# Sums of weights by adding transfers in three units of an output projection

## The chip, the cores and the metric

The kernel runs on one core of a Trainium2 chip. The metric is the device time of one execution in microseconds (us), as the median of a few runs. Beside it stands one execution that was recorded instruction by instruction; every duration below comes from that record. Engines are named as the profile names them: PE multiplies matrices (PEld loads its weights), DVE is the vector engine, ACT the scalar engine, POOL the GpSimd engine, SP the engine that does nothing here but issue transfers. Transfers from SP stand in queue q1, those from POOL in queue q0, and both are carried out by the same 16 DMA engines. A transfer issued from POOL can add to what lies in its destination instead of overwriting it; here it is called an adding transfer.

## The reference, cut to what matters

Two layers on a sequence of 512 rows of width 2048: one of forgetting attention, one of retention. The change lies in the last step of the second layer, the projection of the gated retention output (512 x 4096) to 512 x 2048, which goes with the residual into a LayerNorm:

```python
def retention_branch(x, w_in, w_out):
    ...
    y = o * jax.nn.silu(gate)
    return jnp.einsum('bse,ed->bsd', y, w_out)
...
        h = layer_norm(DEEPNORM_ALPHA * h + y, ln_gain[i], ln_bias[i])
```

All values are float32.

## The kernel before

**Seven products.** Each large matrix product is cut into units. A unit of the wide kind multiplies 512 rows of activations by a 2048 x 1024 piece of weights. Both are cut into quarters (11, 12, 21, 22), and the unit makes seven products of quarters or of sums of quarters, p1 to p7, instead of eight (Strassen's scheme in Winograd's form). On the side of the weights p1 needs w11, p5 needs w11 + w12, p6 needs w11 + w12 + w22, p4 needs w11 + w12 + w22 + w21, p7 needs w12 + w22, p2 takes w21 and p3 takes w22. The first four form a chain: each is the one before plus one more quarter. The sums and forms of the activations are made elsewhere.

**Blocks.** Each product is done in four blocks c = 0 to 3, so a unit has 28. A block's weights are 128 x 1024 float32 (512 KB). To reach float32 accuracy, `split` (L303 to L306) makes two reduced parts of them: ACT writes w_h (L305), DVE writes w_l = w - w_h (L306). Three pairs of these tiles exist. PE then does 12 matmuls of 128 x 512 for the block (L310 to L312), three for each of four places.

**The chain in a block.** `Block.load` (L539) loads w11 of chain c into a tile w_q (L545) and the further quarters into tiles w_raw or room (L551), all from SP. `Block.add` (L553) lets DVE add: for p5, p6 and p4 it does w_q = w_q + the quarter (L565), for p7 it adds two raw tiles (L560). There are four w_q tiles (ring q, given back by the split of p4) and three raw tiles (ring st; a fourth, room, until unit 16). A p2 block leaves its w21 to p4 of the same c, so w21 is loaded once for both.

**The order.** The instructions are written out by a planner. `Order.slot` (L186) handles one block: it loads as far as nine blocks ahead while the rings have room, adds three blocks ahead, splits two blocks ahead, multiplies, and then lets side tasks (sums of results, stores, loads of activation forms) go on as far as a budget of DVE and ACT time allows. Every engine's queue and both transfer queues follow this written order. The order of the products in a unit is ORDER (L55): p1 and p5 take turns, p5 one block behind (p1 0, p1 1, p5 0, p1 2, p5 1, p1 3, p5 2, p5 3), then p6, then p3 and p7 in turns, then p2 and p4 in turns. The last unit of the kernel has the order EARLY (L57) and already makes some sums by adding transfers: w21 is added onto w_q for p4 (L598), and w22 onto w12 in a tile v_sum for p7 (L481, L483).

**Where it lies.** The output projection is units 14 to 17 (L1807, L1809, L1874, L1876), two halves of the 4096 columns of y by two halves of the 2048 columns of the result. The units go on without a break: by the time of the DVE instruction that ends p2 (L450) unit 14 runs from about 2032 to 2120 us of the record, unit 15 to 2202, unit 16 to 2279, unit 17 from there to the end. Beside unit 14 and 15 runs the end of the last retention head (its forms of y are stored and added by POOL in `give_forms`, L806), and `fetch_forms` (L830) brings forms of y back from memory (y_raw, L844) until into unit 16. Units 14 and 15 add the residual (z_res) and store z_half (L1797, L1798), which units 16 and 17 load again.

Of the kernel before, what the change touches and what calls it, by code (L numbers as in the profile page):

```python
# [15 lines left out]
ALU = mybir.AluOpType  # L16
# [36 lines left out]
FIRST = (("p2",), ("p1",))  # L53
REST = (("p5",), ("p6",), ("p3", "p7"), ("p4",))
ORDER = (("p1", "+p5"), ("p6",), ("p3", "p7"), ("p2", "p4"))  # L55

EARLY = (("p1",), ("p5",), ("p2", "p6"), ("p3",), ("p7",), ("p4",))  # L57

# [29 lines left out]
class Order:  # L88
# [17 lines left out]
    def give(self, ring, after=0):  # L106
        if after:
            self.later.append((self.now + after, ring))
        else:
            self.free[ring] += 1  # L110
# [120 lines left out]
def trunk(ctx: ExitStack, tc: tile.TileContext, xq, x, fb_f, columns, wf_in, narrow, wide, ln_g, ln_b, rot, decay,  # L231
# [132 lines left out]
    class Unit:  # L364
# [3 lines left out]
        def __init__(self, w, n, sink, rows=True, u2="k0", p1="k0"):  # L368
            self.w, self.n, self.sink, self.rows, self.u2, self.p1 = w, n, sink, rows, u2, p1
            self.wide = w is wide  # L370
            self.shape = [P, 2, 512] if self.wide else [P, 4, 256]
            self.blocks = 8 // self.shape[1]
            self.tags = None
            self.early = False
            self.bank, self.kept, self.chain, self.lent, self.summed = {}, {}, {}, {}, {}
            self.left = {p: self.blocks for p in FORM}
            self.kept_w, self.of = {}, {}
# [106 lines left out]

            spawn(steps(), 0)

        def run(self, order=ORDER, then={}, leaves=False, last=False):


            self.early = order is EARLY  # L490
            self.leaves, self.last = leaves, last
            order = blocks_of(self.blocks, *order)

            i = order.index(("p3", self.blocks - 1))
            if order[i + 1:i + 3] == [("p7", self.blocks - 1), ("p4", 0)]:
                order[i:i + 2] = order[i + 1], order[i]
            for i, (p, c) in enumerate(order):
                shares = i + 1 < len(order) and order[i + 1] == (SHARES.get(p), c)
                shared = i > 0 and order[i - 1] == ({"p7": "p3", "p4": "p2"}.get(p), c)
                turned = p == "p7" and order[i + 1] == ("p3", c) or p == "p3" and order[i - 1] == ("p7", c)  # L500
                e = (0,) if last and p == "p4" else (0, 1)
                o.push(Block(self, p, c, e, shares, shared, then.get(i), then.get(p), turned))
            for c in range(4 if last else 0):
                o.push(Block(self, "p4", c, (1,), False, False, None, None))

    class Block:
        before = None

        def __init__(self, unit, p, c, e, shares, shared, then_block, then_product, turned=False):
            self.u, self.p, self.c, self.e = unit, p, c, e  # L510
            self.shares, self.shared = shares, shared
            self.then_block, self.then_product = then_block, then_product
            self.done = False
            u = unit
            self.chain = p in ("p1", "p5") and c not in u.chain
            if self.chain:
                u.chain[c] = None
            self.again = e == (1,)
            self.sums = u.early and p in ("p7", "p4")
            self.quarter = None  # L520

            self.turned = turned
            if not self.sums and not shared and p != "p1" and not (turned and p == "p3"):
                self.quarter = {"p2": "21", "p3": "22", "p4": "21", "p5": "12", "p6": "22", "p7": "12"}[p]
            if p == "p7" and shared:
                self.quarter = "12"
            assert p != "p7" or shared or turned or self.sums
            u.of[p, c] = self

        @property  # L530
        def follows(self):

            p = {"p5": "p1", "p6": "p5", "p4": "p6"}.get(self.p)
            return -1 if p is None or self.sums or self.again else self.u.of[p, self.c].at

        def rings(self):
            return dict(q=int(self.chain), st=int(self.quarter is not None) + int(self.turned and self.p == "p7"))
# [15 lines left out]
        def add(self):  # L553

            u, p, c = self.u, self.p, self.c
            if p in ("p2", "p3") and self.shares:
                u.lent[p, c] = self.t
            if p == "p7" and not self.sums:
                other = u.lent["p3", c]
                nc.vector.tensor_add(self.t, self.t, other)  # L560
                if not self.turned:
                    end_raw(u.lent.pop(("p3", c)))
            elif p in ("p5", "p6", "p4") and not self.sums:
                t = u.lent.pop(("p2", c)) if self.shared else self.t
                nc.vector.tensor_add(u.chain[c], u.chain[c], t)  # L565
                end_raw(t)
            else:
                return 0.0
            return 1.14

        def split(self):
            u, p, c = self.u, self.p, self.c
            if self.again:
                self.w = u.kept_w[c]
                return False
            if self.sums:
                raw = u.summed.pop((p, c))
            elif p in ("p1", "p5", "p6", "p4"):
                raw = u.chain[c]
            else:  # L580
                if self.turned and p == "p3":
                    self.t = u.lent.pop((p, c))
                raw = self.t
            if u.last and p == "p4":
                if c % 2 == 0:
                    u.wide_w = [sb8(f"w_{j}", home["a12" if c == 0 else "s2"][i], F32R)
                                              for i, j in enumerate("hl")]
                self.w = u.kept_w[c] = [t[:, c % 2 * 2:c % 2 * 2 + 2] for t in u.wide_w]
            else:
                self.w = [pool.tile(u.shape, F32R, name=f"w_{j}", tag=f"w_{j}", bufs=3) for j in "hl"]  # L590
            split(raw, *self.w)
            if raw is getattr(self, "t", None) and not self.shares:
                end_raw(raw)
            if p == "p4":
                give("q")
            if u.early and p == "p6":
                u.summed["p4", c] = raw
                nc.gpsimd.dma_start(raw.rearrange("p a b -> p (a b)"), u.source("21", c), accum_op=ALU.add)  # L598
            return True
# [1204 lines left out]
        return sink, steps  # L1804

    sink, steps = add_half(0, 2)
    Unit(wide, 14, sink, u2="in1", p1="y0").run(then={"p6": lambda s=steps: spawn(s(), 1)})  # L1807
    sink, steps = add_half(1, 2)
    Unit(wide, 15, sink, u2="k2").run(leaves=True, then={0: lambda s=steps: spawn(s(), 1), **fetch_while(2)})  # L1809

    gb = []

# [58 lines left out]
    half = lambda s, c: z_half[s, c]  # L1871
    spawn(join_room(), 0)
    sink, steps = add_z(0, 1, half, "order")
    Unit(wide, 16, sink, u2="k2").run(then={0: lambda s=steps: spawn(s(), 1)})  # L1874
    sink, steps = add_z(1, 1, half, "early")
    Unit(wide, 17, sink, u2="k2").run(EARLY, then={0: lambda s=steps: (spawn(s(), 1), spawn(biases_there(), 0)), "p2": lambda: spawn(last_gains(), 0),  # L1876
                                          "p3": lambda: [spawn(x) for x in (first_stores(), last_stores(2), last_stores(3))]}, last=True)
# [52 lines left out]
```

## Time and profile before

| | us |
|---|---|
| median of 3 runs | 2389.52 (2388.37 to 2389.93) |
| the recorded execution | 2388.19 |
| its span, first to last instruction | 2386.4 |
| TensorE clock granted in it, share of full | 0.995 |

In the lines of the profile, L is a line of the kernel, `out<-in` are the tiles by their names in the program, x is a count. In a row of windows each engine has its busy time and the number of its instructions, and the last three numbers are the granted clock, the mean busy share of the 16 DMA engines (it can come out somewhat over 1) and the rate in GB/s. A row of waits names who stood still, for whom, for how long in total, how many times, and the longest. A row of issues has the count, the size of one transfer and the median time from its issue to its landing. PE is drawn with pipelined matmuls, so its idle time is what counts, not its busy time.

### The profile page before, as it was taken

The numbers are of one execution on the slowest core, as the hardware profiler recorded it, in microseconds if no ns is written. First come the engines' busy times: TensorE is split into PE (matmuls) and PEld (weight loads), VectorE is DVE, ScalarE is ACT, GpSimd is POOL, SyncE is SP. The second block draws the span as 40 slices with busy tenths as digits, with TensorE's granted clock in tenths as the row PEclk, the third lists the DMA queues.
The fourth block names the chain that finished last, engine by engine and source line by source line (L and its number), as shares of the span: only waits on it lengthen the run. The fifth ranks groups of instructions, "written<-read, shape, count | busy, mean of one in ns | idle before, by whom it ended". The sixth has DMA issues, their size and how long they took to land.

```text
span 2386.4 us, 34361 instructions
## 1 busy us (share of the span) xinstructions
PE 2320.9 (97%) x13144; PEld 2016.2 (84%) x13144; DVE 1892.1 (79%) x2480; ACT 1223.0 (51%) x1777; POOL 150.4 (6%) x236
## 2 busy tenths in 40 slices
PE   9999999999999999999999999999999999999995
PEld 9888798798799778788989898988889898777784
DVE  5888778778765655677888888888888889988887
ACT  4546556555554534564454535454545446544533
POOL 0000000000000000000010101010101001011002
PEclk9999999999999999999999999999999999999998
DMA  6355444544544457556675857575655659689778
GB/s 225 123 196 175 163 161 165 183 161 159 190 153 147 135 194 253 190 177 200 203 239 189 247 192 219 198 206 181 212 195 195 211 169 273 212 267 300 238 245 191
DMA packets 185140, 473.26 MB, mean 198 GB/s; under 512 B 18032, under 2 KB 63232, under 8 KB 184464
## 3 DMA queue, kind: packets, MB, share of 16 engines
q1 hardware_dynamic: 161440, 403.68, 50.8%
q0 software_dynamic: 23536, 67.39, 10.7%
q8 instruction: 103, 1.69, 0.3%
q14 instruction: 61, 0.50, 0.1%
HBM read 413.30 MB, written 61.91 MB: 199 GB/s over the span
## 4 chain that ended last, share of the span: by engine, by line
PE 57%; DVE 8%; issue 3%; DMA 3%; ACT 3%; POOL 0%; ACTq 0%; SPq 0%; DVEq 0%; POOLq 0%
PE acc L311 17%; PE acc L312 17%; PE acc L310 17%; DVE w_l L306 3%; ACT w_h L305 2%; PE mmp L310 1%; DMA w_raw<-in_wide 1%; PE mmp L311 1%; PE mmp L312 1%; DVE w_q L565 1%; DMA v_sum<-in_wide 1%; PE mmp L1202 1%; PE mmp L1736 0%; DMA y_s<-ny 0%; DVE z L1835 0%
## 5 line engine op out<-in xcount | busy, mean ns | idle before, releaser
L310 PE MATMUL acc<-w_h,a 128*128 128x512 f32 (+1 forms) x1616 | 581.7, 360 | 5.5 <-DVE p L460 2.9
L311 PE MATMUL acc<-w_l,a 128*128 128x512 f32 (+1 forms) x1616 | 575.9, 356 | 3.7 <-DVE w_l L306 3.7
L312 PE MATMUL acc<-w_h,a 128*128 128x512 f32 (+1 forms) x1616 | 575.6, 356 | 0.0
L305 ACT ACTIVATE w_h<-w_q 128x1024 fp32r<-128x1024 f32 x344 | 363.9, 1059 | 406.3 <-DVE w_q L565 229.2
L306 DVE TENSOR_TENSOR w_l<-w_raw,w_h 128x1024 fp32r<-128x1024 f32 x337 | 411.6, 1222 | 200.9 <-ACT w_h L305 199.6
L305 ACT ACTIVATE w_h<-w_raw 128x1024 fp32r<-128x1024 f32 x337 | 356.3, 1059 | 378.1 <-PE acc L312 171.2
L306 DVE TENSOR_TENSOR w_l<-w_q,w_h 128x1024 fp32r<-128x1024 f32 x344 | 420.1, 1222 | 93.9 <-ACT w_h L305 86.7
L311 PE MATMUL acc<-w_l,s 128*128 128x512 f32 (+1 forms) x1344 | 485.5, 361 | 9.1 <-DVE w_l L306 8.9
L310 PE MATMUL acc<-w_h,s 128*128 128x512 f32 (+1 forms) x1344 | 489.3, 364 | 1.8 <-ACT w_h L305 1.6
L312 PE MATMUL acc<-w_h,s 128*128 128x512 f32 (+1 forms) x1344 | 483.9, 360 | 0.0
L310 PEld LDWEIGHTS acc<-w_h,a 128*128 128x128 f32 x1616 | 305.5, 189 | 48.8 <-issue 4.2
L311 PEld LDWEIGHTS acc<-w_l,a 128*128 128x128 f32 x1616 | 305.7, 189 | 47.7 <-DVE w_l L306 7.0
L312 PEld LDWEIGHTS acc<-w_h,a 128*128 128x128 f32 x1616 | 305.4, 189 | 44.0
L311 PEld LDWEIGHTS acc<-w_l,s 128*128 128x128 f32 x1344 | 254.4, 189 | 51.5 <-DVE w_l L306 16.6
L310 PEld LDWEIGHTS acc<-w_h,s 128*128 128x128 f32 x1344 | 254.4, 189 | 38.0 <-ACT w_h L305 2.1
L312 PEld LDWEIGHTS acc<-w_h,s 128*128 128x128 f32 x1344 | 254.2, 189 | 38.1
L565 DVE TENSOR_TENSOR w_q<-w_q,w_raw 128x1024 f32<-128x1024 f32 x218 | 265.4, 1220 | 9.6 <-DMA w_raw<-in_wide 7.2
L310 PE MATMUL acc<-a,w_h 128*128 128x256 f32 x464 | 131.5, 283 | 1.3 <-ACT w_h L305 1.3
L312 PE MATMUL acc<-a,w_l 128*128 128x256 f32 x464 | 131.6, 284 | 0.8 <-DVE w_l L306 0.8
L311 PE MATMUL acc<-a,w_h 128*128 128x256 f32 x464 | 131.3, 283 | 0.0
L312 PE MATMUL acc<-s,w_l 128*128 128x256 f32 x448 | 126.8, 283 | 0.0
L311 PE MATMUL acc<-s,w_h 128*128 128x256 f32 x448 | 126.7, 283 | 0.0
(244 smaller groups left out, 2942.5 us busy)
## 6 DMA issues: line engine op xcount, KB each, us to landing
w_raw<-in_wide SPq DMA_DIRECT2D x343, 512.0 KB, 3.9
w_raw<-in_narrow SPq DMA_DIRECT2D x146, 512.0 KB, 3.9
w_q<-in_wide SPq DMA_DIRECT2D x60, 512.0 KB, 4.3
room<-in_wide SPq DMA_DIRECT2D x45, 512.0 KB, 4.4
w_q<-in_narrow SPq DMA_DIRECT2D x26, 512.0 KB, 4.3
y_s<-ny POOLq DMA_DIRECT2D x48, 256.0 KB, 7.3
y_s<-y POOLq DMA_DIRECT2D x40, 256.0 KB, 6.2
room<-in_narrow SPq DMA_DIRECT2D x16, 512.0 KB, 4.6
```

The lines of the kernel that those rows point to most:

```text
L305: nc.scalar.activation(h, src, AF.Copy)
L306: nc.vector.tensor_sub(l, src, f32(h))
L310: nc.tensor.matmul(ps, a[0], b[0], start=start, stop=False, skip_group_check=True)
L311: nc.tensor.matmul(ps, a[0], b[1], start=False, stop=False, skip_group_check=True)
L312: nc.tensor.matmul(ps, a[1], b[0], start=False, stop=stop, skip_group_check=True)
L565: nc.vector.tensor_add(u.chain[c], u.chain[c], t)
L1202: nc.tensor.matmul(ps[:, k * P:], vh[:, k], pT[:, k, k * P:], start=k == 0, stop=k == ST - 1)
```

## The change

Units 14, 15 and 16 get a new flag `adds`. With it the order is ADDS: four blocks of p1, then four of p5, four of p6, then p3 and p7 in turns, then p2 and p4 in turns. Blocks of p5, p6 and p4 load no quarter and make no sum on DVE. Instead, as soon as a block of p1, p5 or p6 has been split, POOL issues an adding transfer of 512 KB that brings the next quarter of the chain (12, 22 or 21) onto the same w_q tile, and the split of the next product of that chain waits for its landing. p2 still loads w21 for itself; p4 no longer takes it over. Units 1 to 13 and 17 and the first layer are left as they are.

```diff
+ADDS = (("p1",), ("p5",), ("p6",), ("p3", "p7"), ("p2", "p4"))
...
-            self.early = order is EARLY
+            self.early, self.adds = order is EARLY, adds
+            if adds:
+                order = ADDS
...
-                shares = i + 1 < len(order) and order[i + 1] == (SHARES.get(p), c)
-                shared = i > 0 and order[i - 1] == ({"p7": "p3", "p4": "p2"}.get(p), c)
+                shares = i + 1 < len(order) and order[i + 1] == (SHARES.get(p), c) and not (self.adds and p == "p2")
+                shared = i > 0 and not (self.adds and p == "p4") and order[i - 1] == ({"p7": "p3", "p4": "p2"}.get(p), c)
...
+            self.comes = u.adds and p in ("p5", "p6", "p4")
...
-            if not self.sums and not shared and p != "p1" and not (turned and p == "p3"):
+            if not self.sums and not self.comes and not shared and p != "p1" and not (turned and p == "p3"):
...
-            elif p in ("p5", "p6", "p4") and not self.sums:
+            elif p in ("p5", "p6", "p4") and not self.sums and not self.comes:
...
+            elif u.adds and p in ("p1", "p5", "p6"):
+                q = {"p1": "12", "p5": "22", "p6": "21"}[p]
+                nc.gpsimd.dma_start(raw.rearrange("p a b -> p (a b)"), u.source(q, c), accum_op=ALU.add)
...
-    Unit(wide, 14, sink, u2="in1", p1="y0").run(then={"p6": lambda s=steps: spawn(s(), 1)})
+    Unit(wide, 14, sink, u2="in1", p1="y0").run(adds=True, then={"p6": lambda s=steps: spawn(s(), 1)})
...
-    Unit(wide, 15, sink, u2="k2").run(leaves=True, then={0: lambda s=steps: spawn(s(), 1), **fetch_while(2)})
+    Unit(wide, 15, sink, u2="k2").run(adds=True, leaves=True, then={0: lambda s=steps: spawn(s(), 1), **fetch_while(2)})
...
-    Unit(wide, 16, sink, u2="k2").run(then={0: lambda s=steps: spawn(s(), 1)})
+    Unit(wide, 16, sink, u2="k2").run(adds=True, then={0: lambda s=steps: spawn(s(), 1)})
```

More of the change, by code (lines that the diff above doesn't have):

```diff
@@ L373, in __init__ @@
             self.tags = None
-            self.early = False
+            self.early = self.adds = False
             self.bank, self.kept, self.chain, self.lent, self.summed = {}, {}, {}, {}, {}
@@ L485, in sum_ahead, with run @@
             spawn(steps(), 0)
-        def run(self, order=ORDER, then={}, leaves=False, last=False):
-            self.early = order is EARLY
+        def run(self, order=ORDER, then={}, leaves=False, last=False, adds=False):
+            self.early, self.adds = order is EARLY, adds
+            if adds:
+                order = ADDS
             self.leaves, self.last = leaves, last
@@ L533, in follows @@
             p = {"p5": "p1", "p6": "p5", "p4": "p6"}.get(self.p)
-            return -1 if p is None or self.sums or self.again else self.u.of[p, self.c].at
+            return -1 if p is None or self.sums or self.comes or self.again else self.u.of[p, self.c].at
         def rings(self):
```

## The prediction

> **What bounds the kernel now.** First the page: which engine is full, and whether the last tenth differs from the rest.
>
> ```profile
> span 2386.4 us, 34361 instructions
> ...
> PE 2320.9 (97%) x13144; PEld 2016.2 (84%) x13144; DVE 1892.1 (79%) x2480; ACT 1223.0 (51%) x1777; POOL 150.4 (6%) x236
> ...
> DVE  5888778778765655677888888888888889988887
> ...
> PEclk9999999999999999999999999999999999999998
> DMA  6355444544544457556675857575655659689778
> ```
>
> PE bounds the span and runs at full clock. The changed units lie in slices 34 to 38 of the 40. There DVE is at its densest (8 and 9 tenths), and so are the DMA engines (6, 8, 9, 7). So I read that stretch in windows, one for each of units 14, 15 and 16, and one for the start of 17.
>
> ```profile
> 2032.00:2120.00 88.00, 85.59 (x375) 68.68 (x374) 81.30 (x104) 45.26 (x48) 4.18 (x7) 1.00 0.72 233
> 2120.00:2202.00 82.00, 80.37 (x357) 65.89 (x356) 66.35 (x62) 40.52 (x43) 12.33 (x18) 1.00 0.93 286
> 2202.00:2279.00 77.00, 74.91 (x324) 59.74 (x323) 70.64 (x67) 40.47 (x40) 3.22 (x6) 1.00 0.71 230
> 2279.00:2300.00 21.00, 21.00 (x95) 17.38 (x94) 20.74 (x23) 9.42 (x9) 0.00 (x0) 1.00 0.71 251
> ```
>
> PE is idle for 2.4, 1.6 and 2.1 us in the three units, 6.1 us in 247. DVE is at 92%, 81% and 92%. The DMA engines are busy for 0.72 x 88 = 63.4, 0.93 x 82 = 76.3 and 0.71 x 77 = 54.7 us. What PE waits for there stands in the waits of PE from 2032 to 2279:
>
> ```profile
> PE acc L311 <- DVE w_l L306: 3.1, 6, 0.7
> PE acc L310 <- DVE p L460: 2.9, 2, 1.5
> ```
>
> All of it is DVE running late: 6.0 us in eight waits. The two of 1.5 us are those of p4's first block for the bank of p7, which DVE still has to read (L460) while sums and splits stand ahead of that read in its queue.
>
> **What goes.** The groups of DVE instructions in the same stretch:
>
> ```profile
> L306 DVE TENSOR_TENSOR w_l<-w_q,w_h 128x1024 fp32r<-128x1024 f32 x48 | 58.6, 1222 | 10.8 <-ACT w_h L305 9.9
> ...
> L565 DVE TENSOR_TENSOR w_q<-w_q,w_raw 128x1024 f32<-128x1024 f32 x30 | 36.5, 1221 | 1.5 <-DMA w_raw<-in_wide 1.2
> ...
> L565 DVE TENSOR_TENSOR w_q<-w_q,room 128x1024 f32<-128x1024 f32 x6 | 7.3, 1221 | 0.1
> ```
>
> The 30 + 6 = 36 sums of L565 (12 in each unit) leave DVE: 36 x 1.22 = 43.9 us. On the path that sets the end this can be worth only what PE waited for, 6.0 us; the rest was covered by PE's own work. Reordering p1 and p5 issues nothing and costs nothing by itself: p1 then leaves four blocks instead of two before p6 takes its bank again. I take the whole 6.0 us as the ceiling of the gain. From SP's queue go the loads of p5 and p6, 8 in a unit, 24 in all; p4 had none of its own.
>
> **What comes.** 12 adding transfers in a unit, 36 in all, on POOL's queue. Their price on the DMA engines is to be read where few others run, in unit 17, which has such transfers already. The first two rows are windows with adding transfers, the last one with plain loads; below them stand the queues of the first and the third.
>
> ```profile
> 2320.00:2323.00 3.00, 2.33 (x11) 1.73 (x10) 2.93 (x3) 1.86 (x2) 0.00 (x0) 1.00 1.07 214
> 2338.00:2342.00 4.00, 3.34 (x15) 2.77 (x16) 3.39 (x4) 1.33 (x3) 2.55 (x4) 1.00 1.06 208
> 2316.00:2319.00 3.00, 3.00 (x15) 2.48 (x14) 0.48 (x1) 0.00 (x0) 1.42 (x2) 1.00 1.02 412
> ```
>
> ```profile
> q0 software_dynamic: 168, 0.63, 105.3%
> q1 hardware_dynamic: 5, 0.02, 1.5%
> ```
>
> ```profile
> q1 hardware_dynamic: 330, 1.22, 99.7%
> q0 software_dynamic: 4, 0.01, 2.1%
> ```
>
> With nearly all packets adding ones (168 of 173), the engines are full at 214 GB/s; with plain ones they are full at 412. One transfer of 524 KB (512 x 1024 bytes) costs 524 / (214 / 1.07) = 2.62 us of all 16 engines if it adds, and 524 / (412 / 1.02) = 1.30 if it doesn't. A unit therefore gets 12 x 2.62 - 8 x 1.30 = 21.0 us more transfer time. These are prices of the engines' time, bounded on both sides by rows: below by a plain load (1.30), above by what an adding transfer gets when a plain stream runs beside it, from 2328 to 2333:
>
> ```profile
> q0 software_dynamic: 178, 0.66, 66.4%
> q1 hardware_dynamic: 189, 0.71, 37.6%
> ```
>
> The two queues get as many packets each, and the adding ones 0.66 MB in 5 us, so one lasts 524 / 132 = 4.0 us there. I take 2.62, since it was measured on the same kind of transfer (weights onto a tile) with the engines full, and keep 1.30 and 4.0 for the range.
>
> The Trainium skill ("Collectives: The Full Stack", section "The bandwidth ceiling: the fold count and why AG ≠ RS ≠ AR") says that a transfer that adds reads two sources on one ring and so runs at half the rate of a copy. The rows agree (2.62 against 1.30). [...]
>
> **Does it fit?** New transfer time is the old plus 21.0: 84.4 us in the 88 of unit 14, 97.3 in the 82 of unit 15, 75.7 in the 77 of unit 16. The densest stretch of before shows how much a window can hold; beside it stand the fronts of units 16 and 14, from p1's first splits to p6's last:
>
> ```profile
> 2155.00:2202.00 47.00, 45.37 (x199) 36.95 (x198) 37.96 (x36) 22.45 (x23) 6.71 (x10) 1.00 1.06 322
> 2200.00:2232.00 32.00, 30.30 (x130) 23.67 (x129) 29.91 (x29) 17.82 (x19) 3.22 (x6) 1.00 0.91 288
> 2031.00:2064.00 33.00, 31.97 (x138) 25.16 (x137) 30.34 (x29) 18.90 (x20) 0.56 (x1) 1.00 0.77 252
> ```
>
> A share of 1.06 is held for 47 us, so I call 1.06 full. Unit 15 holds 82 x 1.06 = 86.9 and is asked for 97.3: **10.4 us over**. Units 14 and 16 fit as a whole (93.3 and 81.6), but the adding transfers come early in a unit: 8 of them, those for p5 and p6, must land before p6's last split. Front of unit 16: 0.91 x 32 = 29.1, less 8 loads (10.4), plus 8 x 2.62 = 21.0 makes 39.7 in 32 x 1.06 = 33.9: **5.8 over**. Front of unit 14: 0.77 x 33 = 25.4, and with the same 10.6 more 36.0 in 35.0: **1.0 over**. Not all of the front's traffic is urgent. In unit 16's front there are
>
> ```profile
> y_raw<-y_s SPq DMA_DIRECT2D x6, 256.0 KB, 5.3
> ...
> y_raw<-y_a SPq DMA_DIRECT2D x4, 256.0 KB, 6.7
> ```
>
> ten loads of forms of y. By the code the last forms of `fetch_while` (s3, a12, a22) are wanted only in the back half; I count five of ten as free to wait, an estimate of 5 x 0.65 = 3.3 us at the plain rate. Added loss: 10.4 + 5.8 + 1.0 - 3.3 = 13.9 us.
>
> Of the 6.0 us of gain, those in windows that are now full of transfers don't count, since the sums above start from the window's length with its stalls: 1.6 in unit 15 (PE's idle time) and 1.7 in the front of unit 16 (32 - 30.30). That leaves 2.7. **Sum: 13.9 - 2.7 = +11.2 us** on the recorded 2388.19. That execution lies 1.3 below the median of the runs, within their spread, so I put the sum on the median: 2389.5 + 11.2 = 2400.7.
>
> **The new wait.** The split of p5 c now waits for a transfer that starts only after the split of p1 c, and p6 c for one after p5 c. The rows for one link of that chain: POOL's issue and landing (unit 17, L598), ACT's and DVE's part of the split, and PE's time for a block.
>
> ```profile
> L598 POOL DMA_DIRECT2D w_q<-in_wide x4: 916/963/1170, 2304.1 to 2323.8; - x4
> ...
> DMA to landing us min/median/max: 6.8/9.7/11.5
> ```
>
> ```profile
> L305 ACT ACTIVATE w_h<-w_q 128x1024 fp32r<-128x1024 f32 x344 | 363.9, 1059 | 406.3 <-DVE w_q L565 229.2
> ```
>
> ```profile
> 2260.00:2318.00 58.00, 58.00 (x257) 47.81 (x256) 3.98 (x5) 2.06 (x2) 1.00 0.69 225
> ```
>
> The last row is of the matmuls on acc alone: 257 in 58 us without a pause, 0.226 each, 12 x 0.226 = 2.71 for a block and 10.8 for the four from p1 c to p5 c. A link is landing plus 1.06 + 1.22 of split: 9.1 at the shortest, 12.0 at the median, 13.8 at the longest. Three pairs of w_h and w_l let a split start two blocks (5.4 us) before its own block, so it can be done 5.4 - 2.3 = 3.1 early. Two links at the median lose 2 x 1.2 = 2.4 of these 3.1 and PE feels nothing; at the longest they lose 6.0 and PE stands 2.9 us in each unit. Behind a waiting split, ACT and DVE hold in order the next splits and the sums of results; PE waits for those. On POOL, the new issues stand in line with the stores that wait for DVE and ACT:
>
> ```profile
> POOL z_half L1798 <- DVE z_in L1797: 123.6, 13, 58.6
> ```
>
> That wait is long because the store has little ahead of it; DVE does its z_in before the split that comes after it, so a new issue behind such a store is no later than its own split would be, and I cost it at nothing. The cover is that common order; without it an issue would be up to one z_in late (0.7 us).
>
> **The rivals.** *It fits after all.* Loads are issued blocks ahead, from 2155 to 2202 the engines were at 1.06 and PE lost only 1.6 us. If raw tiles and the lead of 3.1 us swallow the excess too, what is left is the gain: -6.0, 2383.5. For it: the median link loses only 2.4. Against it: unit 15 lacks 10.4 us of transfer time, more than any lead. It decides as long as links stay below 10.8 + 3.1 / 2 = 12.4 us. *Gain and excess cancel.* Waiting forms and stores slip into gaps elsewhere and half of the loss goes: 13.9 / 2 - 2.7 = +4.3, and down to -4: about 2390. *The queues share.* If plain traffic stands beside the adding transfers in every front, eight take 8 x 4.0 = 32 after a fixed part of 6.8 - 2.62 = 4.2, and the split 2.3: 38.5 us, where 11 blocks and the lead give 29.8 + 3.1 = 32.9. Loss 5.6 in each unit, 16.8; with unit 15's 10.4 and less 2.7 it is +24.5: 2414. Against it: only part of a front has a full plain queue (share 0.77 and 0.91 before, with the 8 loads that go). *Adding is free.* If an adding transfer took only the time of a plain one, a unit would get (12 - 8) x 1.30 = 5.2 us more, 81.5 in unit 15 against 86.9, and the front would get none: -6.0, 2383.5. The rows at 214 and 412 GB/s speak against it. [...]
>
> **How the numbers follow.** About 0.2% (4.8 us) is what a measurement of this kernel can tell from no change. Forecast, unit 15 short of transfer time, 2400.7 (its own range 2395 to 2406): 0.41. Queues share: 0.17. Cancel: 0.19. Fits: 0.19. Free add: 0.04. Slower 0.58, same 0.19, faster 0.23. The range goes from the gain alone, 2383, to 2412, short of the end of the shared queues; the larger gains and losses outside it hold some 0.15.
>
> **What would show it.** Right: the DMA share in unit 15 at 1.0 or more over the whole unit; waits of ACT's w_h (L305) for adding transfers on w_q, and of PE for w_h and w_l behind them, most in the fronts of 15 and 16; landings above 12 us; L565 gone from the stretch and DVE near 75%; the two waits for L460 gone. Wrong: unit 15 no longer than 82 us, or landings that stay below 12 with a busy share under 1.

## The result and the profile after

| | before | after |
|---|---|---|
| median of 4 runs, us | 2388.94 (2387.13 to 2389.93) | 2418.23 (2417.39 to 2422.42) |
| the recorded execution, us | 2388.19 | 2417.39 |
| its span, us | 2386.4 | 2415.3 |

The kernel became slower: the ratio of after to before is 1.0127, with an interval of 1.0109 to 1.0145, or 29.3 us. That is the direction of the forecast and outside its range (2383 to 2412). First the page of the kernel after, in the same lines as before:

```profile
span 2415.3 us, 34380 instructions
...
PE 2333.4 (97%) x13144; PEld 2022.4 (84%) x13144; DVE 1851.8 (77%) x2444; ACT 1222.2 (51%) x1777; POOL 182.0 (8%) x272
...
DVE  5888778678665556678988888888888889746677
...
PEclk9999999999999999999999999999999999999997
DMA  6365544554545366556675857575757578999877
```

Two readings. DVE is lighter by the 36 sums (2480 less 2444 instructions), and its 8s and 9s near the end have become 7, 4, 6, 6, while the DMA engines now stand at 9 in three slices. And PE's 13144 matmuls are the same in number, but its busy time has grown from 2320.9 to 2333.4, 12.5 us, and its idle time from 65.5 to 81.9 (span less busy), 16.4 us. The two make the 28.9 us by which the span grew. So more than two fifths of the loss is not waiting; most of that is matmuls that themselves ran slower, as shown below.

Where it lies is seen by the DVE instruction that ends p2 in each unit. Before it stands at 2032.4, 2120.1, 2201.8 and 2279.3 us, after at 2030.9, 2120.8, 2212.7 and 2306.3. Unit 14 is 2.3 us longer (90.0 against 87.7), unit 15 10.1 (91.8 against 81.7), unit 16 16.1 (93.6 against 77.5), and all behind it 2.0; the start is 1.5 earlier. These stretches do not hold quite the same work: between these instructions lie 372, 354 and 325 matmuls before and 382, 336 and 336 after. At the 0.226 us of a matmul in the prediction's row, unit 15 after has 4.1 us less to do, units 14 and 16 have 2.3 and 2.5 us more. For equal work unit 14 is not longer at all, unit 15 is 14.2 us longer and unit 16 13.6. The windows of the three units after (columns as in the prediction's windows: length, busy time of PE, PEld, DVE, ACT, POOL with counts, granted clock, DMA share, GB/s):

```profile
2031.00:2121.00 90.00, 86.51 (x384) 69.84 (x383) 67.51 (x92) 47.69 (x54) 19.41 (x25) 1.00 0.98 264
2121.00:2213.00 92.00, 83.70 (x339) 66.00 (x338) 52.53 (x49) 38.29 (x39) 18.61 (x25) 0.94 0.98 261
2213.00:2306.00 93.00, 81.69 (x335) 63.96 (x334) 59.01 (x56) 40.69 (x40) 13.63 (x18) 0.94 0.87 239
```

PE is idle for 3.5, 8.3 and 11.3 us where it was idle for 2.4, 1.6 and 2.1, and its mean clock is 0.94 in units 15 and 16, where it was 1.00. The DMA engines stand near full for all of units 14 and 15. DVE fell to 75%, 57% and 63%.

Now who is late. The waits of PE in unit 15 and in unit 16:

```profile
PE acc L313 <- DVE w_l L308: 4.4, 4, 2.0
PE acc L312 <- ACT w_h L307: 3.2, 2, 1.8
PE acc L312 <- DVE p L462: 0.6, 1, 0.6
```

```profile
PE acc L312 <- ACT w_h L307: 6.5, 2, 6.2
PE acc L312 <- ACT u L417: 2.4, 1, 2.4
PE acc L313 <- DVE w_l L308: 2.2, 4, 0.8
```

It is the splits that are late. The two waits of 1.5 us for p4's bank (L460 before, L462 after) have shrunk to one of 0.6. One step further back, the waits of ACT in unit 15 and in unit 16 (those for the DMA):

```profile
ACT w_h L307 <- DMA w_q<-in_wide: 18.2, 7, 4.4
...
ACT ny L1750 <- DMA z_half<-z_in: 4.7, 1, 4.7
ACT a L307 <- DMA y_raw<-y_a: 2.8, 1, 2.8
```

```profile
ACT w_h L307 <- DMA w_q<-in_wide: 11.8, 5, 3.9
ACT a L307 <- DMA y_raw<-y_a: 7.4, 2, 4.2
ACT s L307 <- DMA y_raw<-y_s: 7.4, 1, 7.4
```

In unit 15 the splits wait for the adding transfers: each of the seven waits for w_q ends with the landing of one from L604. In unit 16 the longest single wait is not for one of these but for a plain load, y_raw, a form of y. The timeline of ACT shows what stands behind it in ACT's written order (start, length, and in brackets the idle time before it and whom it waited for):

```profile
2240.68 1.06 ACT L307 ACTIVATE w_h<-w_q 128x1024 fp32r<-128x1024 f32 x1 [2.98 <-DMA w_q<-in_wide]
2249.09 1.06 ACT L307 ACTIVATE s<-y_raw 128x1024 fp32r<-128x1024 f32 x1 [7.36 <-DMA y_raw<-y_s]
2250.06 1.00 ACT L417 ACTIVATE p<-acc 128x1024 f32<-128x1024 f32 x1
2250.96 1.99 ACT L307 ACTIVATE w_h<-w_q 128x1024 fp32r<-128x1024 f32 x2
```

The split of a form of y holds ACT from 2241.7 to 2249.1; the next split of weights comes at 2250.96, and PE's matmuls on it at 2252.1, after the wait of 6.2. What the DMA engines did in that stretch, by queue (packets, MB, share of 16 engines), from 2237 to 2252:

```profile
q0 software_dynamic: 628, 2.31, 77.1%
q1 hardware_dynamic: 653, 1.50, 28.7%
```

Together they fill the engines (105.8%), and each gets about as many packets as the other (628 against 653), whoever's bytes are wanted. The even count belongs to this stretch: from 2213 to 2237, with mostly 512-byte packets in the plain queue, it was 1055 against 4329. The adding queue moves 2.31 MB in 15 us, so one of its transfers lasts 524 / 154 = 3.4 us and not 2.62 (over the whole front, 2213 to 2252, it moved 6.04 MB, some stores among them, which is the same rate); a plain queue moved 1.22 MB in 3 us when it was alone and 1.50 in these 15. The landings of y_raw in units 15 and 16, first before, then after:

```profile
DMA to landing us min/median/max: 4.4/6.6/9.5
```

```profile
DMA to landing us min/median/max: 4.1/8.8/23.5
```

The slower matmuls are seen on PE itself. The timeline at the first wait of unit 15:

```profile
2144.44 0.49 PE L312 MATMUL acc<-w_h,s 128*128 128x512 f32 x1 [1.36 <-ACT w_h L307]
2145.70 0.50 PE L313 MATMUL acc<-w_l,s 128*128 128x512 f32 x1 [0.77 <-DVE w_l L308]
...
2147.19 0.63 PE L314 MATMUL acc<-w_h,s 128*128 128x512 f32 x1
2147.62 0.63 PE L312 MATMUL acc<-w_h,s 128*128 128x512 f32 x1
2148.04 0.63 PE L313 MATMUL acc<-w_l,s 128*128 128x512 f32 x1
```

After two waits that make 2.1 us the matmuls follow each other every 0.43 us instead of 0.23: the granted clock is half. The record of the clock has such stretches at 2146.18, 2156.42 and 2180.31 (3.41 us each), 2248.58 (10.24) and 2364.63 (6.83), each behind a wait. Before it had one of 3.41 us at 128.6, long ahead of the changed units, and both have one in the tail.

### The profile page after: what moved, and what is told of

Read it like the earlier page. It is cut to its first block, busy times and chain, and to the rows that moved or that the text cites. A ratio compares the mean times of both kernels' runs of the same rounds, so it can differ in the third digit from the quotient of the medians.

```text
span 2415.3 us, 34380 instructions
## 1 busy us (share of the span) xinstructions
PE 2333.4 (97%) x13144; PEld 2022.4 (84%) x13144; DVE 1851.8 (77%) x2444; ACT 1222.2 (51%) x1777; POOL 182.0 (8%) x272
## 4 chain that ended last, share of the span: by engine, by line
PE 57%; DVE 7%; DMA 4%; issue 3%; ACT 3%; SPq 1%; POOL 1%; ACTq 0%; DVEq 0%; POOLq 0%
PE acc L313 17%; PE acc L314 17%; PE acc L312 17%; DVE w_l L308 3%; DMA w_raw<-in_wide 2%; ACT w_h L307 2%; PE mmp L312 1%; PE mmp L313 1%; PE mmp L314 1%; DMA y_raw<-y_a 1%; PE mmp L1211 1%; DVE w_q L571 1%; SPq L853 1%; DMA w_q<-in_wide 1%; SPq L557 1%
## 5 line engine op out<-in xcount | busy, mean ns | idle before, releaser
L307 ACT ACTIVATE w_h<-w_q 128x1024 fp32r<-128x1024 f32 x344 | 363.7, 1059 | 407.1 <-DVE w_q L571 170.2
L307 ACT ACTIVATE w_h<-w_raw 128x1024 fp32r<-128x1024 f32 x337 | 356.0, 1058 | 375.9 <-PE acc L314 177.8
L571 DVE TENSOR_TENSOR w_q<-w_q,w_raw 128x1024 f32<-128x1024 f32 x188 | 228.9, 1220 | 7.9 <-DMA w_raw<-in_wide 5.7
```

The source lines that it names most:

```text
L307: nc.scalar.activation(h, src, AF.Copy)
```

## The experiments

The first theory was the price on the DMA engines: an adding transfer takes twice the time of a plain one, so the stretch runs out of transfer time. Three rivals stood against it: **links** (a split waits for a landing that starts only after the split before it, whatever the transfer costs), **order** (the new order of the products, and the loads and stores moved by it), and, for how the price reaches PE, **turns** (adding packets delay other queues' small ones). In the diffs the lines are those of the kernel after unless said otherwise. Every result is a median with its ratio to the kernel before (2388.5 to 2389.7 in these comparisons), interval in brackets. "Units" are the lengths of 14, 15 and 16 in the recorded execution; before they are 87.7, 81.7, 77.5, after 90.0, 91.8, 93.6.

### The price, the order and the links

**small_add** brings only 128 of the 1024 columns by each adding transfer, so the sums are left incomplete.

```diff
-nc.gpsimd.dma_start(raw.rearrange("p a b -> p (a b)"), u.source(q, c), accum_op=ALU.add)
+nc.gpsimd.dma_start(raw.rearrange("p a b -> p (a b)")[:, :128], u.source(q, c)[:, :128], accum_op=ALU.add)
```

> The changed kernel, but each of the 36 new adding transfers brings only the first 128 of 1024 columns (64 KB instead of 512); the other columns of the sums for p5, p6 and p4 are left out. Order, waits and number of transfers stay. Three theories are on trial. Engine time: the 2.62 us of the 16 engines that an adding transfer takes is what makes the rest late. Turns: the two queues take turns packet by packet, so the 512-byte packets of y_raw on q1 each wait for a 4 KB adding packet, y_raw lands late, ACT waits for it in order and PE behind ACT. Links: issue on POOL, landing and split are longer than four blocks, whatever the bytes. Engine time and turns both expect the loss of 29 us to go and the gain of DVE's lighter load to appear: 2381 to 2389 us, no drop of the granted clock in units 14 to 16. Links expects 2400 us or more.

**plain_over** moves the same bytes with the same waits, but overwrites.

```diff
-nc.gpsimd.dma_start(raw.rearrange("p a b -> p (a b)"), u.source(q, c), accum_op=ALU.add)
+nc.gpsimd.dma_start(raw.rearrange("p a b -> p (a b)"), u.source(q, c))
```

> The changed kernel, but the 36 new transfers overwrite w_q instead of adding to it, same bytes, same queue, same waits; the sums for p5, p6 and p4 are left out (each gets the last quarter alone). Engine time expects 1.30 us instead of 2.62 for each, unit 15 at 76.3 + 5.2 us of transfers in 82, so 2383 to 2392 us. Turns expects that y_raw is still held up, half as much (a plain 4 KB packet took 163 to 170 ns, an adding one 328): 2392 to 2405 us. Links expects 2405 us or more, since issue and fixed latency are the same.

**order_only** has the order ADDS in the three units and leaves the sums on DVE, as before. Units 15 and 16 are edited like unit 14:

```diff
-    Unit(wide, 14, sink, u2="in1", p1="y0").run(adds=True, then={"p6": lambda s=steps: spawn(s(), 1)})
+    Unit(wide, 14, sink, u2="in1", p1="y0").run(ADDS, then={"p6": lambda s=steps: spawn(s(), 1)})
```

> The kernel before with the new order of the products in units 14, 15 and 16 (four blocks of p1, then four of p5), and all sums on DVE as before: no new transfer. If the order itself costs nothing, 2386 to 2391 us, the same as before; if the order has a part in the loss, over 2394 us.

Measured: small_add 2379.81 us, 0.9963 [0.9949, 0.9977]; plain_over 2382.3, 0.9975 [0.9964, 0.9985]; order_only 2392.07, 1.0012 [1.0003, 1.0021]. The windows of units 15 and 16 in small_add, then in plain_over:

```profile
2122.40:2198.80 76.40, 76.40 (x338) 63.01 (x337) 52.37 (x49) 38.08 (x39) 18.39 (x25) 1.00 0.88 242
2198.80:2274.90 76.10, 76.10 (x337) 63.04 (x336) 59.26 (x56) 40.99 (x40) 13.86 (x18) 1.00 0.73 222
```

```profile
2119.90:2196.30 76.40, 76.40 (x337) 62.99 (x336) 52.37 (x48) 38.17 (x38) 13.71 (x24) 1.00 0.94 314
2196.30:2276.00 79.70, 77.56 (x337) 62.68 (x336) 59.31 (x57) 41.06 (x41) 9.74 (x18) 1.00 0.82 281
```

PE never stops in small_add (76.40 of 76.40) and for 2.1 us in plain_over. Both have every wait and every issue of the change. The landings of these 36 transfers, first in the kernel after, then in plain_over:

```profile
DMA to landing us min/median/max: 5.8/9.0/12.8
```

```profile
DMA to landing us min/median/max: 3.5/6.9/8.6
```

A plain transfer lands 2.1 us earlier at the median, and with that the links close. So the links by themselves fall as a rival, the order costs about 3 us (0.7 to 5.0 by its interval), and what is left is that the transfers add. The gain of taking the sums off DVE is shown too: 6.5 us with plain transfers of the same bytes, 9 in small_add, which moves an eighth of them. It is what the change would bring if adding were cheap.

**plain_twice** is plain_over with a copy of the same quarter into spare memory behind each transfer: about the engine time of an adding transfer, without any adding.

```diff
+spare = [dram.tile([P, 1024], F32, name=f"spare{c}") for c in range(4)]
...
-nc.gpsimd.dma_start(raw.rearrange("p a b -> p (a b)"), u.source(q, c), accum_op=ALU.add)
+nc.gpsimd.dma_start(raw.rearrange("p a b -> p (a b)"), u.source(q, c))
+nc.gpsimd.dma_start(spare[c], u.source(q, c))
```

> The run with overwriting transfers (sums for p5, p6 and p4 left out; 2382 us), and behind each of the 36 a copy of the same quarter into spare memory on the same queue, which nobody waits for. So q0 is given about twice the engine time, near that of adding, but in packets half as long. If the engines' time is what costs, it loses like the changed kernel: 2405 to 2425 us. If the length of an adding packet in the turns with q1 is what costs, it stays within 2383 to 2398 us.

Measured: 2411.45 us, 1.0096 [1.0083, 1.011]; units 88.2, 91.0, 91.9. The loss is back to three quarters, in the same two units, with ACT standing for y_raw and for w_q. The waits of ACT in units 15 and 16 together (both of those for y_s are in unit 16):

```profile
ACT s L307 <- DMA y_raw<-y_s: 16.9, 2, 11.2
ACT w_h L307 <- DMA w_q<-in_wide: 8.6, 4, 2.8
```

So a loss of this kind needs no adding; as many more bytes in POOL's queue do it too. What the run does not do is to part the engines' time from long packets in the turns. The copies were expected in packets half as long as adding ones, but in the record they went in packets of 32 KB that took 1.21 us each, where an adding packet of 4 KB took 0.33.

### Which unit, which product

**only14**, **only15** and **only16** make the change in one unit; the two others keep the old order and their sums; for only14 the edit is

```diff
-    Unit(wide, 15, sink, u2="k2").run(adds=True, leaves=True, then={0: lambda s=steps: spawn(s(), 1), **fetch_while(2)})
+    Unit(wide, 15, sink, u2="k2").run(leaves=True, then={0: lambda s=steps: spawn(s(), 1), **fetch_while(2)})
...
-    Unit(wide, 16, sink, u2="k2").run(adds=True, then={0: lambda s=steps: spawn(s(), 1)})
+    Unit(wide, 16, sink, u2="k2").run(then={0: lambda s=steps: spawn(s(), 1)})
```

> The change in unit 14 alone. Unit 14 had the lightest transfers of the three in its window (63 us in 88). By the sum of engine time it fits (84 in 93): 2385 to 2390 us. If late forms or stores hold ACT there too, 2391 to 2398 us.

> The change in unit 15 alone. Unit 14 alone cost nothing, unit 16 alone 22 us, all three 29. If the losses add up, unit 15 alone costs 7 to 12 us: 2396 to 2401. If unit 16 in the changed kernel was partly relieved or burdened by unit 15, it is outside that; by the sum for unit 15 (10.4 us of engine time over, less its stalls) 2399.

> The change in unit 16 alone; units 14 and 15 as before. In the changed kernel unit 16 took 16 us more than before, and its transfers rose by 27 us of engine time, 6 more than the 21 that its own adding transfers bring. If its loss is its own (eight adding transfers that must land in its front, beside y_raw), it stays nearly whole: 2399 to 2406 us. If most of it is backlog handed on from unit 15, 2389 to 2396 us.

Measured: only14 2388.49, 0.9997 [0.9987, 1.0006]; only15 2402.41, 1.0059 [1.0044, 1.0074]; only16 2410.18, 1.0089 [1.0073, 1.0104]. The window of the changed unit in each:

```profile
2034.10:2123.30 89.20, 86.78 (x385) 70.06 (x384) 68.72 (x93) 47.76 (x53) 19.46 (x25) 1.00 1.00 284
```

```profile
2120.50:2214.30 93.80, 84.02 (x353) 67.32 (x351) 53.32 (x50) 40.58 (x43) 24.48 (x32) 0.93 1.06 289
```

```profile
2202.80:2299.00 96.20, 80.63 (x325) 63.79 (x325) 59.50 (x58) 39.45 (x40) 13.95 (x18) 0.91 0.83 229
```

Unit 14 holds its transfers, as the sum of the prediction had it. Unit 15 is full over its whole length (1.06 in the mean). PE stands still there for 4.3 and 4.4 us, and each time ACT, ahead of the split that PE needs, waits in its written order for a store in POOL's queue to land:

```profile
ACT ny L1750 <- DMA y_s<-ny: 7.2, 1, 7.2
...
ACT ny L1750 <- DMA z_half<-z_in: 4.7, 1, 4.7
```

Unit 16 is the surprise: it loses most, with a share of 0.83 over the unit, so it is not short of transfer time as a whole. PE waits 8.5 us there at once, behind `ACT a L307 <- DMA y_raw<-y_a`, 10.5 us in one wait. The losses of the single units, 0 + 13 + 22, make more than the 29 of all three.

**p5p6** makes the sums of p5 and p6 by adding transfers and leaves p4's on DVE, with w21 shared with p2 again (first diff); **p4_only** does the reverse, in the old order (second diff).

```diff
-                shares = i + 1 < len(order) and order[i + 1] == (SHARES.get(p), c) and not (self.adds and p == "p2")
-                shared = i > 0 and not (self.adds and p == "p4") and order[i - 1] == ({"p7": "p3", "p4": "p2"}.get(p), c)
+                shares = i + 1 < len(order) and order[i + 1] == (SHARES.get(p), c)
+                shared = i > 0 and order[i - 1] == ({"p7": "p3", "p4": "p2"}.get(p), c)
...
-            self.comes = u.adds and p in ("p5", "p6", "p4")
+            self.comes = u.adds and p in ("p5", "p6")
...
-            elif u.adds and p in ("p1", "p5", "p6"):
-                q = {"p1": "12", "p5": "22", "p6": "21"}[p]
+            elif u.adds and p in ("p1", "p5"):
+                q = {"p1": "12", "p5": "22"}[p]
```

```diff
-            if adds:
-                order = ADDS
...
-            self.comes = u.adds and p in ("p5", "p6", "p4")
+            self.comes = u.adds and p == "p4"
...
-            elif u.adds and p in ("p1", "p5", "p6"):
-                q = {"p1": "12", "p5": "22", "p6": "21"}[p]
+            elif u.adds and p == "p6":
+                q = "21"
```

> New order; only the sums for p5 and p6 come by adding transfers, p4 is summed by DVE from the quarter that it shares with p2, as before. 8 adding transfers take the place of 8 loads in a unit: 8 x (2.62 - 1.30) = 10.5 us more engine time, the same as in the run with p4 alone, but all of it in the front and on the tight links. If the front decides, most of the loss of the whole change is here: 2400 to 2414 us. If the unit's total decides, about the same as the run with p4 alone: 2386 to 2394 us.

> Old order; in units 14 to 16 only the sum for p4 comes by an adding transfer, issued after p6's split, 10 blocks or more before it is needed; p5 and p6 are summed by DVE as before. Each unit gets 4 x 2.62 = 10.5 us more engine time and gives DVE 4 sums less. If the whole unit's engine time decides, unit 15 (76.3 + 10.5 = 86.8 in 82, limit 86.9) is at its limit and loses a little, the others gain: 2386 to 2394 us. If only the tight links p1 to p5 to p6 hurt, nothing is late and the gain of up to 6 us shows: 2382 to 2386 us.

Measured: p5p6 2404.55, 1.0069 [1.0055, 1.0082]; p4_only 2410.64, 1.0093 [1.0079, 1.0107], against what was expected: p4's sum has the most time before its split, and yet four adding transfers a unit cost 22 us. Its units are 87.3, 95.7 and 86.4. PE's longest wait in unit 15 is 7.8 us, for ACT, and ACT there stood for three stores that had not yet left their buffers:

```profile
ACT ny L1748 <- DMA y_s<-ny: 6.2, 1, 6.2
ACT y L1747 <- DMA y_a<-y: 6.2, 1, 6.2
ACT ny L1748 <- DMA y_s<-y: 5.7, 1, 5.7
```

These stores of forms of y go through POOL's queue, as the adding transfers do, and stand behind them: one of y_a, issued 0.6 us after a transfer for p4, landed after 9.6 us, where the stores of y_a in unit 15 landed after 3.0 to 5.7 before. Before, ACT waited 4.8 us in all for such stores there. An adding transfer that is itself in no hurry delays others that are.

**late4** issues the transfer for p4 only after p7's split, out of the way of the front; **p4_pool** is the kernel before with p4's sum made by POOL in units 14 to 16.

```diff
-            elif u.adds and p in ("p1", "p5", "p6"):
-                q = {"p1": "12", "p5": "22", "p6": "21"}[p]
-                nc.gpsimd.dma_start(raw.rearrange("p a b -> p (a b)"), u.source(q, c), accum_op=ALU.add)
+            elif u.adds and p in ("p1", "p5", "p7"):
+                q = {"p1": "12", "p5": "22", "p7": "21"}[p]
+                nc.gpsimd.dma_start(u.chain[c].rearrange("p a b -> p (a b)"), u.source(q, c), accum_op=ALU.add)
```

```diff
+                if p == "p4" and self.u.w is wide and 14 <= self.u.n <= 16:
+                    nc.gpsimd.tensor_add(u.chain[c], u.chain[c], t)
+                    end_raw(t)
+                    return 0.0
```

> The changed kernel, but the adding transfer for p4 is issued after the split of p7 of the same c, 5 to 8 blocks later than after that of p6, and still 7 or more blocks ahead of p4. Same transfers, same bytes. If the front of a unit is short because 12 adding transfers of 2.62 us crowd it and not the 8 urgent ones, most of the loss in unit 16 goes: 2398 to 2408 us. If the total of a unit decides, or the urgent links alone, nothing changes: 2414 to 2420 us.

> The kernel before, old order, but in units 14 to 16 the four sums for p4 are made by POOL as an instruction (GpSimd adds two tiles in on-chip memory) instead of DVE: no transfer is added. DVE gives up 12 sums of 1.22 us at the place where PE waits twice 1.5 us for L460. If the new sum ends within the blocks of lead that it has and DVE isn't slowed, 2383 to 2387 us; if POOL is slow, or slows DVE beside it, 2389 to 2410 us.

Measured: late4 2421.32, 1.0138 [1.0117, 1.0159], no better; that p4's transfers crowd the front was a wrong idea. p4_pool 2401.75, 1.0057 [1.0044, 1.0069]: PE then waits up to 4.8 us for p4's bank, and the sum is cheaper on DVE.

### How the price reaches PE

**after_2k** and **before_2k** lay the tile y_raw out so that its loads have packets of 2 KB instead of 512 bytes, in the kernel after and before.

```diff
-                t = pool.tile([P, 8, 256], F32, name="y_raw", tag=home[VIA[n]][0] if n in VIA else "g0")
+                t = pool.tile([P, 2, 8, P], F32, name="y_raw", tag=home[VIA[n]][0] if n in VIA else "g0")
...
-                        nc.sync.dma_start(t[:, c:c + 4, e * P:(e + 1) * P], yf[i][n][:, e, c:c + 4])
+                        nc.sync.dma_start(t[:, e, c:c + 4], yf[i][n][:, e, c:c + 4])
```

> The changed kernel with the forms of y (y_raw, loaded for units 14 to 17) laid out in the tile as they lie in memory, so that they come in packets of 2 KB instead of 512 bytes; the splits read them by a rearranged view. Turns expects that y_raw needs a quarter of the turns, lands within 10 us instead of up to 23, ACT's waits for y_raw (10 us in unit 14, 15 us in unit 16) shrink to under 4, and the time falls to 2395 to 2407 us. Engine time expects the same bytes in the same time, 2412 to 2420 us.

> The kernel before with y_raw in packets of 2 KB instead of 512 bytes, as in the run with the change; no adding transfers. Without adding packets in the other queue the turns matter little: 2385 to 2390 us, at most 3 us faster. If the 7 us that the 2 KB packets gave the changed kernel come from the transfers of y_raw alone and not from the turns beside adding packets, 2380 to 2384 us.

**act_queue** issues the second set of y_raw from ACT instead of SP.

```diff
-                        nc.sync.dma_start(t[:, c:c + 4, e * P:(e + 1) * P], yf[i][n][:, e, c:c + 4])
+                        (nc.scalar if i == 2 else nc.sync).dma_start(t[:, c:c + 4, e * P:(e + 1) * P], yf[i][n][:, e, c:c + 4])
```

> The changed kernel with the second set of forms of y (y_raw) loaded by ACT's queue instead of SP's, so that weights on q1 no longer stand behind them and each queue has its own turn. ACT issues 28 transfers more. If weights behind slow y_raw loads make a good part of the loss, 2400 to 2410 us; if the engines' time alone decides, 2414 to 2424.

Measured: after_2k 2411.44, 1.0095 [1.0081, 1.0108]; before_2k 2389.14, 1.0000 [0.9991, 1.0009]; act_queue 2421.34, 1.0138 [1.0121, 1.0155]. Larger packets help the kernel after by 7 of its 29 us and the kernel before by nothing; y_raw still lands up to 25.7 us after its issue. Another queue for them helps nothing. So the small packets of y_raw are a part of the cause, not the whole.

**only16_free** is only16 with the second set of y_raw loaded but not waited for (the split reads a constant tile). **only16_noy** leaves these loads out as well, and **after_noy** does so in the full change (the first two lines of the diff are not in only16_free). In all three the activations of that set are replaced by a constant.

```diff
-                for e in range(2):
+                for e in range(2 if i < 2 else 0):
...
-                split_form(n, at[n, c][0][:, c:c + 4], c, c + 4)
+                if i == 2:
+                    src = ident[:, None, None, :].to_broadcast([P, 4, 2, P])
+                    split(src, *(x[:, c:c + 4].rearrange("p k (e n) -> p k e n", e=2) for x in forms[n]))
```

> The change in unit 16 alone, and the second set of forms of y (for units 16 and 17) is loaded as before but not read: ACT and DVE split a constant tile instead, in the same places and sizes, so nobody waits for these loads until their tiles are used again. The results of units 16 and 17 are wrong by that. All transfers stay. The run with unit 16 alone took 2410 us, 22 over the kernel before, with PE idle for 8.5 us in one piece behind ACT. If what costs is that ACT and DVE stand in order behind a late y_raw, most of it goes: 2389 to 2397 us. If the adding transfers' own links (w_q landing late) cost it, it stays: 2403 to 2412 us.

> The run with the change in unit 16 alone and the constant tile in place of the second set of forms (2406 us), and now the loads of that set (y_raw, 28 transfers of 256 KB in units 15 and 16) are left out too; results of units 16 and 17 are wrong by that. If adding transfers are late only because they share the engines, each falls from 3.4 us to near 2.7 and the loss goes: 2383 to 2391 us. If the chain with 2.62 us each is too tight by itself, 2398 to 2406 us.

> The changed kernel (units 14 to 16) with the same loads of forms left out and a constant tile split in their place. Unit 15 then has about 84 us of transfers in 82 instead of 97, unit 16 about 63 in 77. If sharing is the cause, at most unit 15 loses a little: 2384 to 2396 us. If the chain is too tight by itself, 2404 to 2414 us.

Measured: only16_free 2406.21, 1.0073 [1.0059, 1.0087]; only16_noy 2392.44, 1.0015 [1.0006, 1.0025]; after_noy 2406.66, 1.0073 [1.0058, 1.0088]. Not waiting for y_raw saves some 4 of 22 us (the intervals of only16 and only16_free overlap): my theory that ACT's wait for y_raw is itself the main route falls, for the next late ones take its place. The waits for the DMA in only16_free, with ACT's for the quarter of p5, p6, p4 and DVE's for that of p7:

```profile
ACT w_h L307 <- DMA w_q<-in_wide: 16.4, 7, 3.7
DVE w_raw L566 <- DMA w_raw<-in_wide: 12.8, 4, 6.4
```

Leaving the loads out brings 22 down to 3. It takes away their time on the engines, their 512-byte packets and their place ahead of weights in q1 all at once. The window of unit 16 in only16_noy:

```profile
2198.10:2281.40 83.30, 79.13 (x336) 63.57 (x335) 59.11 (x57) 40.28 (x40) 13.95 (x18) 0.98 0.80 216
```

So it is the traffic beside the adding transfers in unit 16's front that makes somebody late. That it is a matter of the order which transfer that is, is my reading; no run tests it. In the full change leaving them out saves 12 of 29 (units 90.8, 89.1, 85.3). 17 remain; units 15 and 16 are still 7.4 and 7.8 us longer than before, and in unit 15 ACT's waits for w_q are as long as with the loads (17.6 us against 18.2). How those 17 divide between the stores, the links and the clock no run here tells.

## Why the prediction was right in direction and wrong in size

**Right.** The gain from PE's waits: it counted 6.0 us, plain_over shows 6.5. (As a ceiling it is not safe: small_add shows 9, with an interval from 5.5, and its recorded units are 9.4 us shorter in all, where PE's idle time before was 6.1.) The price of 2.62 against 1.30 as the cause: plain_over takes the loss away, plain_twice brings three quarters of it back. Unit 15 as short of transfer time: only15 has the term in the clearest form, a share of 1.06 held for 93.8 us. Its size, 10.4 us against the 10.1 by which the unit grew, agrees by luck, as shown below. Unit 14 fits. The order costs little. Of the signs named, L565 is gone, ACT's w_h waits for w_q (18.2 us in unit 15), and the L460 waits are all but gone; DVE fell further than "near 75%" in units 15 and 16. The share in unit 15 is 0.98 and not over 1.0 in the full change, and landings are 9.0 at the median and pass 12 in two of 36 (12.6 and 12.8).

**The step that failed** is "Does it fit?", in unit 16: "Front of unit 16 ... 5.8 over", less "five of ten as free to wait ... 3.3", which made 2.5. Measured are 16.1, or 13.6 for equal work. The step took 2.62 us for a transfer and let the plain loads of y step aside. Nothing stepped aside: the engines carried both queues at once, so an adding transfer lasted 3.4 us in the front, and the last of the eight for p5 and p6 landed 34.9 us after the first issue (29.6 in unit 14, 36.2 in unit 15), where 11 blocks and the lead, less the split, allow 29.8 + 3.1 - 2.3 = 30.6. The loads that were to be free to wait landed up to 23.5 us after their issue (9.5 before), and ACT, which takes its work in the written order, held the splits of weights behind them. Without these loads the 22 us of only16 were 3. The prediction had written this down as the rival of shared queues: 36.2 us for the eight, 2414 in all. It gave it 0.17, on the ground that the share before was only 0.91 in that front. That ground was a mean over 32 us of a kernel whose queues were not yet full; the 10.6 us of new transfer time is what fills them.

The Trainium skill ("DMA: Bandwidth & Descriptors", section "Queues, rings and completion order") says that each DMA engine goes round its queues packet by packet, a packet being a group of descriptors. The row of 628 against 653 packets agrees with even turns, as did the prediction's row of 178 against 189, which spoke against "free to wait"; whether a packet of the profile is one of that section no row here shows.

**A term that was missing.** The working has PE at full clock after each wait. The half-clock stretches outside the tail last 3 x 3.41 + 10.24 + 6.83 = 27.3 us, in 4.7 of which PE stood still; half of the other 22.6 is 11.3 us (5.1 in unit 15, 3.2 in unit 16, 3.0 in unit 17). The kernel before has one stretch of 3.41 us, at 128.6, that the kernel after hasn't, which takes 1.7 off; in the tail, where PE mostly stands still, the difference is under 0.2. That leaves about 9.7 of the 12.5 us by which PE's busy time grew; for the rest I have no cause. This is read from the record; no run changed the clock alone.

So unit 15's agreement is luck: of its 10.1 us, 6.7 are idle time and the half clock makes 5.1, of which the step knew nothing, and the 18 matmuls that no longer lie in it hide 4.1; 2.4 I can't place. In unit 16 idle time and clock make 9.2 + 3.2 = 12.4 of the 16.1, and the 11 matmuls that it has more make 2.5; the other 1.2 I can't place either.

**Also wrong** was to cost the new issues on POOL at nothing. For their place in POOL's order that may hold; for the queue behind it, p4_only shows that stores of y wait for adding transfers ahead of them, 18 us in three waits of ACT, and only15 shows the same of stores of y and z_half, 12 us in two.

## What to carry to other kernels

When work goes from an engine to the transfers, sum the engines' time by the stretch in which it must land, and count every byte there as urgent: the queues share the engines, and a load that could wait delays an engine that takes its work in order. In a chain of transfers, price each at what it gets beside a full queue (3.4 to 4.0 us here), not at what it gets alone (2.62). And where some 2 us of PE's waiting fall together, add the half clock that can follow.

## What the runs showed of the hardware

**Adding.** A packet of 4 KB took 0.33 us of its engine when it added (from 2320 to 2323 before) and 0.16 when it didn't (2316 to 2319). The same bytes on the same tiles land after 9.0 us (median) when they add and after 6.9 when they overwrite, and the whole kernel differs by 36 us between the two (2418.2 and 2382.3).

**The clock.** The half-clock stretches are whole multiples of 3.41 us, and their starts in the kernel after lie on a grid of 3.413 us: they are apart by 10.24, 23.89, 68.27 and 116.05 us, which is 3, 7, 20 and 34 times that. By the record of the kernel after, what counts is PE's waiting within one step of this grid. In the changed units and behind them, steps with 1.98, 2.12 (1.36 + 0.77), 2.41, 2.77 and 1.87 us of it were each followed by half clock; steps with 1.63 and 1.42 were not. A wait of 2.42 us at 2264.64, longer than that of 1.98, lay across an edge of the grid, 1.00 on one side and 1.42 on the other, and was not followed. Nor were the 1.4, 1.5 and 1.64 us of before. The Trainium skill ("TensorE: Matmul & The Clock Gate", section "Part 1: The HAM clock gate (the "warmup" mystery)") has a free-running window of 3413 ns and half rate after an idle one. Grid and rate agree; but here some 2 us of waiting within one step was enough, and the matmuls between the two waits did not prevent it.
